# Inverses turned by VectorE, the mixer's output product on whole fp32 weights, and S5's input projections in pairs of row groups

## The chip, the cores and the metric

One NeuronCore of a Trainium2 chip runs the whole program as one launch. The metric is the time of an execution in device microseconds; lower is better. Before the change the median of three runs is 3645.67 us (3633.72 to 3649.02).

## What is computed

Two transformer blocks for 256 tokens of width 2048, all in fp32. The first is a hybrid mixer (sparse attention and a Mamba2 scan, both 1024 wide, whose results are joined and multiplied by `w_out`) and a product-key expert layer. The second has three branches of width 1024: a gated delta rule, RWKV-7 and a diagonal state-space model (S5). Cut to what the change touches:

```python
# first block: the mixer's output product, [256, 2048] @ [2048, 2048]
return jnp.concatenate([attn, ssm], axis=-1) @ w_out
# second block, S5: the input projections of every group of channels
bu_re = jnp.einsum('gpc,blgc->blgp', bb_re, ug)
bu_im = jnp.einsum('gpc,blgc->blgp', bb_im, ug)
# second block, delta rule: the inverse of a unit lower triangular matrix
t_mat = lax.linalg.triangular_solve(eye + lower, jnp.broadcast_to(eye, lower.shape),
                                    left_side=True, lower=True)
```

RWKV-7 is computed in chunks in the kernel, so it needs inverses of the same kind.

## The kernel before

**Weights in two parts.** A weight tile [128, 1024] is loaded by SyncE into a staging tile (`raw`, four of them, and two named `rawm` in the first block). ScalarE copies it, rounded, into `whi` (L280), VectorE subtracts that from the tile into `wlo` (L284), and TensorE forms three products of rounded operands (`mm3`, L291 to L293: high by high, high by low, low by high) or two where high and low of the activations lie side by side (`mm2`, L299 and L300). There are two pairs of `whi` and `wlo`, and a third while `self.third` names a pool. Such products (fp32r) are one record of TensorE; a product of fp32 operands is two records.

**Streams.** Weight products are generators in `self.queue`. `fill()` advances the first of them by one weight tile; the attention heads, the scans, S5 and the inverses call it between their own steps, so that products of weights stand between them on TensorE. `self.bg` is a second stream: the modulation weights (`ada`), 512 KB tiles that VectorE multiplies by the condition (L355) in the mixer's time. The framework then orders each engine's instructions itself; each engine runs them in that order.

**The mixer's output product** (`mixer`, `tm`). The attention's result is turned into `aT` (`chunk_T`, high part by ScalarE, low part by VectorE, L445) and multiplied by half of `w_out` in four groups of 512 columns, 4 weight tiles each, from 419 to 502 us beside the scan of the state-space half (`ssd`); that half's result is turned into `mT` and multiplied by the other half of the weights. The modulation stream runs beside both.

**S5** (`s5`). For each of 8 groups of 128 channels: the input matrices are turned (`pb`), and for each of four state tiles, which take 32 of those channels each, TensorE forms the real and the imaginary projection (L1729, L1730) in a bank of its own, VectorE rotates them (L1735, L1736), GpSimd joins them (L1737, L1738), VectorE scans (L1741), and `fill` puts two or three weight steps behind it. The pool `sm` has four banks.

**Inverses** (`inverse2`, called 16 times by `rwkv_pair` and 8 times by `gdn_pair`, two at a time through `both`). A call inverts two unit lower triangular matrices side by side, by doubling the block size from 1 to 64. In a step of block size b the off-diagonal blocks (`lb`, masked by GpSimd at L1790) are multiplied by the inverse so far, `Y` (L1805), `Y` is turned by TensorE (L1807), ScalarE copies both to SBUF (L1809), the two are multiplied (L1814), and VectorE subtracts the result from `Y` (L1815). Up to b = 32 `Y` consists of diagonal blocks no larger than 32 x 32 when it is turned. The start (L1798, L1800) turns the blocks of size 1 and subtracts them from the identity.

Of the kernel before, what the change touches and what calls it, by code (L numbers as in the profile page):

```python
# [7 lines left out]
F32 = mybir.dt.float32  # L8
F32R = mybir.dt.float32r
I32 = mybir.dt.int32  # L10
U32 = mybir.dt.uint32
AF = mybir.ActivationFunctionType
ALU = mybir.AluOpType
# [220 lines left out]
class K:  # L234
    def __init__(self, tc, A, at, dbg=None):
        self.tc, self.nc, self.A, self.at, self.dbg_ = tc, tc.nc, A, at, dbg
        self.n = 0
        self.pp, self.queue, self.done, self.bg = [], [], set(), []
        self.bgr, self.bgc = 1.0, 0.0
        self.side, self.later = [], [[] for _ in range(LAG)]  # L240
        self.third, self.ns = None, 0
        self.more, self.nr = None, 0

# [41 lines left out]

    def wt(self, src, n=1024, **kw):
        return self.split(self.raw(src, n), n, **kw)

    def mm3(self, out, shi, slo, mhi, mlo, start, stop):
        mm = self.nc.tensor.matmul  # L290
# [145 lines left out]
    def chunk_T(self, src, dg, hi, lo, scale, half=0):  # L436

        nc = self.nc
        if half == 0:
            self.ctb = self.bank()  # L440
        ps = self.ctb[:, half * S : half * S + S]
        for q in range(2):
            self.turn(ps[:, q * 128 : q * 128 + 128], src[q], dg and dg[q])
        nc.scalar.activation(hi, ps, AF.Copy, scale=scale)
        nc.vector.scalar_tensor_tensor(lo, ps, scale, hi.bitcast(F32), op0=ALU.mult, op1=ALU.subtract)  # L445

    def chunks_T(self, pool, x, cs, dg, hh, hl, scale, shift):

# [156 lines left out]
    def mixer(self, hp, mx, ax, hT, kvT, qT, xs, ev, scr):  # L605
# [31 lines left out]
        self.feed(*[self.cm(A["w1cm"], j, hT, lambda j, ps: ev((2 * NP + j + 8) % 12, ps), ("x", j)) for j in range(12 - 2 * NP)])  # L637
        self.feed(*[self.tm(A["w1z"], g, hT, self.gates(xs[2]), ("z", g)) for g in range(2)])
        atp = tc.alloc_tile_pool(name="atp", bufs=1, side="right")
        aT = [self.t(atp, [128, 8, S], F32R) for _ in range(2)]  # L640
        self.until("t320")
        gate = self.t(mx, [128, 2, 48])
        nc.scalar.activation(gate, vtm[:, :, 256:304], AF.Tanh, scale=0.5)
# [13 lines left out]
        nw = self.cp("attn_norm", "cp2")  # L657
        for c in range(8):
            a = [at[:, q, c * 128 : c * 128 + 128] for q in range(2)]
            self.chunk_T(a, None, aT[0][:, c], aT[1][:, c], nw[:, c : c + 1], c % 2)  # L660
        self.dbg("aTd", aT[0].bitcast(F32))
        ax.release()

        xp = tc.alloc_tile_pool(name="x1p", bufs=1)
# [20 lines left out]

        wo = lambda h: [A["wo1"][8 * g + 4 * h + i] for g in range(4) for i in range(4)]
        for g in range(4):
            self.feed(self.tm(wo(0), g, aT, ev_a, nk=8))
        assert not self.side
        self.until(*[("x", j) for j in range(12 - 2 * NP)])  # L690
        self.flush()
        turn, mT = self.ssd(mx, xs, hp)
        self.drain()
        for g in range(4):
            self.feed(self.tm(wo(1), g, mT, ev_m, nk=8))
        self.fill(3)
        for _ in turn:
            pass
        self.dbg("mTd", mT[0].bitcast(F32))
        self.drain()  # L700
        while self.bg:
            self.step_bg()
# [251 lines left out]
    def ssd(self, mx, xs, hp):  # L954

        nc = self.nc
        V, ACT, PL = nc.vector, nc.scalar, nc.gpsimd
        tri = self.cp("tri", "ca")
        xtm, bc, zs = xs
        dt, acs, acsT, ds = self.sd  # L960
        y = zs
        ss = self.t(mx, [128, 4])

        def scan(g, hg, cbT, py):
            h = g * 8 + hg
            pa = self.bank()
            nc.tensor.matmul(pa[:, 0:256], self.ident[:16, h : h + 1].to_broadcast([16, 128]), acsT, start=True, stop=True)
            seg = self.t(mx, [128, 384], tag="seg", bufs=2)
            ACT.activation(seg[:, 0:256], pa[:, 0:256], AF.Relu, scale=-1.0, bias=acs[:, 0, h : h + 1])
            ACT.activation(seg[:, 256:384], pa[:, 128:256], AF.Relu, scale=-1.0, bias=acs[:, 1, h : h + 1])  # L970
            ACT.activation(seg, seg, AF.Exp, scale=-1.0)
            V.scalar_tensor_tensor(seg[:, 0:256], seg[:, 0:256], dt[:, 0, h : h + 1], cbT[:, 0:256], op0=ALU.mult, op1=ALU.mult)
            V.scalar_tensor_tensor(seg[:, 256:384], seg[:, 256:384], dt[:, 1, h : h + 1], cbT[:, 256:384], op0=ALU.mult, op1=ALU.mult)
            yield
            o = slice(hg * 64, hg * 64 + 64)
            xc = slice(h * 64, h * 64 + 64)
            nc.tensor.matmul(py[0][:, o], seg[:, 0:128], xtm[:, 0, xc], start=True, stop=True)
            nc.tensor.matmul(py[1][:, o], seg[:, 128:256], xtm[:, 0, xc], start=True, stop=False)
            nc.tensor.matmul(py[1][:, o], seg[:, 256:384], xtm[:, 1, xc], start=False, stop=True)
            yield  # L980

        def turns(g, mT):
            nw = self.cp("ssm_norm", "cp2")
            for c in range(4 * g, 4 * g + 4):
                a = [y[:, q, c * 128 : c * 128 + 128] for q in range(2)]
                self.chunk_T(a, None, mT[0][:, c], mT[1][:, c], nw[:, c : c + 1], c % 2)
                if c % 2:
                    yield

        for g in range(2):  # L990
            ps = self.bank()
            Bt, Ct = bc[:, g], bc[:, 2 + g]
            nc.tensor.matmul(ps[:, 0:256], Bt[:, 0:128], Ct, start=True, stop=True)
            nc.tensor.matmul(ps[:, 256:384], Bt[:, 128:256], Ct[:, 128:256], start=True, stop=True)
            cbT = self.t(mx, [128, 384], tag="cbT", bufs=2)
            V.tensor_tensor(cbT[:, 0:256], ps[:, 0:256], tri, op=ALU.mult)
            V.tensor_tensor(cbT[:, 256:384], ps[:, 256:384], tri[:, :128], op=ALU.mult)
            py = [self.bank() for _ in range(2)]
            self.fill()
            gens = [scan(g, hg, cbT, py) for hg in range(8)]  # L1000
            if g:
                gens.insert(2, turn)
            self.weave(gens, 1, 0.17)
            self.until(("z", g))
            for q in range(2):
                c = slice(g * 512, g * 512 + 512)
                t1 = self.t(mx, [128, 512], tag="yd", bufs=2)
                PL.tensor_tensor(
                    t1.rearrange("p (h d) -> p h d", h=8), xtm[:, q, c].rearrange("p (h d) -> p h d", h=8),
                    ds[:, g * 8 : g * 8 + 8, None].to_broadcast([128, 8, 64]), op=ALU.mult,  # L1010
                )
                V.tensor_tensor(t1, py[q], t1, op=ALU.add)
                V.tensor_tensor(y[:, q, c], t1, zs[:, q, c], op=ALU.mult)
                ACT.activation(t1, y[:, q, c], AF.Square, accum_out=ss[:, 2 * q + g : 2 * q + g + 1])
            r = self.rstd(mx, ss[:, g::2], 2, 512.0, 4 * EPS)
            y0, y1 = (y[:, q, g * 512 : g * 512 + 512] for q in range(2))
            ACT.activation(y0, y0, AF.Copy, scale=r[:, 0:1])
            V.tensor_scalar(y1, y1, r[:, 1:2], None, op0=ALU.mult)
            if g == 0:
                self.until(("z", 1))  # L1020
                mT = self.pair(hp, 8, "hh")
            turn = turns(g, mT)
        return turn, mT

# [326 lines left out]
    def tm(self, wd, g, hT, evac, key=None, nk=NK):  # L1351

        hh, hl = hT[:2]
        ps = [self.t(self.acc, [128, 512], tag="acc") for _ in range(2)]
        for kp in range(nk // 2):
            hi, lo = self.wt(wd[g * (nk // 2) + kp])
            yield
            for k in range(2):
                kk = 2 * kp + k
                w = slice(k * 512, k * 512 + 512)  # L1360
                for q in range(2):
                    tk = slice(q * 128, q * 128 + 128)
                    self.mm3(ps[q], hh[:, kk, tk], hl[:, kk, tk], hi[:, w], lo[:, w], kk == 0, kk == nk - 1)
        for q in range(2):
            evac(g, q, ps[q])
        self.done.add(key)

    def step_bg(self):
        while self.bg:
# [320 lines left out]
    def s5(self, pl, u_, yT):  # L1690
# [19 lines left out]
        for j in range(8):  # L1710
# [11 lines left out]
            states = []  # L1722
            for i in range(4):
                sc = 4 * j + i
                P = slice(32 * i, 32 * i + 32)
                cs = self.r2()
                nc.sync.dma_start(cs, self.s5t[sc])
                pu = self.bank()
                nc.tensor.matmul(pu[:, 0:256], bT[P, 0:128], u[P], start=True, stop=True)  # L1729
                nc.tensor.matmul(pu[:, 256:512], bT[P, 128:256], u[P], start=True, stop=True)  # L1730

                w2 = lambda x: x.rearrange("p (w t) -> p w t", w=2)
                co, ns = (cs[:, None, o : o + 256].to_broadcast([128, 2, S]) for o in (0, 256))
# [44 lines left out]
    def inverse2(self, L, res):  # L1778
# [14 lines left out]

        lm, lb = masked(1), masked(2)
        yield
        ps = self.bank()
        for i in range(2):
            nc.tensor.transpose(ps[:, T[i]], lm[:, T[i]], self.ident)  # L1798
        Y = self.r1()
        V.tensor_tensor(v2(Y), id2, v2(ps[:, 0:256]), op=ALU.subtract)  # L1800
        yield
        for b in (2, 4, 8, 16, 32):
            ps = self.bank()
            for i in range(2):
                mm(ps[:, T[i]], lb[:, T[i]], Y[:, T[i]], start=True, stop=True)  # L1805
            for i in range(2):
                nc.tensor.transpose(ps[:, U[i]], Y[:, T[i]], self.ident)  # L1807
            zx = self.r2()
            nc.scalar.activation(zx, ps, AF.Copy)  # L1809
            if b < 32:  # L1810
                lb = masked(2 * b)
            yield
# [500 lines left out]
```

## Time and profile before

| | |
|---|---|
| median of 3 runs | 3645.67 us (3633.72 to 3649.02) |
| the profiled execution | 3638.32 us, span 3636.3 us |
| mean granted TensorE clock | 0.972 |
| TensorE matmul, weight load | 96%, 81% of the span |
| VectorE, ScalarE, GpSimd | 71%, 47%, 11% |
| read from HBM | 673.87 MB, 194 GB/s over the span |

The share of the matmul row holds each record's pipeline tail; how much a record takes from the next is read from the distance of their starts in the timeline. The stages that the change touches: the mixer's output product from about 402 to 565 us, S5 from 2217 to 2545, inverses of RWKV from 2596 to about 3110 and of the delta rule to about 3490.

### The profile page before, as it was taken

Reading aid. Unit: us, or ns where it says so; the run is one execution under the profiler, and the core shown is the slowest. Engines: PE = TensorE matmul, PEld = TensorE weight load, DVE = VectorE, ACT = ScalarE, POOL = GpSimd, SP = SyncE. Lnnn points to the kernel's source line nnn. Section 1 sums busy time; section 2 is a strip of 40 time slices with the busy share of each in tenths; the row PEclk is TensorE's granted clock in tenths of the full one; section 3 lists DMA queues with packets and bytes.
Section 4 is the critical chain, followed back from the end, with each engine's and each line's share of the span. In section 5 each row is a group of like instructions: output and inputs, shape, how many; then the busy total and the mean of one; then the engine's idle time right before and its main releaser. Section 6 shows DMA issues by size and latency. Waiting matters only on the chain. (4 is left out here: it accounts for less than half of the span.)

```text
span 3636.3 us, 53121 instructions
## 1 busy us (share of the span) xinstructions
PE 3473.7 (96%) x19334; PEld 2930.2 (81%) x19334; DVE 2570.2 (71%) x4552; ACT 1692.7 (47%) x2966; POOL 397.2 (11%) x487
## 2 busy tenths in 40 slices
PE   5899988999999999999999998999999999999998
PEld 4888767888998888778887877877888888778887
DVE  7777886798887755565577668989766666665665
ACT  2355544445554444445555554333544445444444
POOL 0000010000000000000000002333223222021310
PEclk7999988999999999999999998999999999999999
DMA  8965776666556865566788755645433433444455
GB/s 334 336 225 194 251 254 209 197 196 202 161 159 207 259 190 188 183 204 206 241 283 285 248 189 202 198 152 188 147 109 112 144 129 106 140 132 151 141 176 189
DMA packets 237298, 710.46 MB, mean 195 GB/s; under 512 B 34091, under 2 KB 61804, under 8 KB 235756
## 3 DMA queue, kind: packets, MB, share of 16 engines
q1 hardware_dynamic: 207564, 672.08, 56.7%
q10 hardware_dynamic: 29472, 34.98, 2.9%
q8 instruction: 152, 2.49, 0.3%
q14 instruction: 110, 0.90, 0.1%
HBM read 673.87 MB, written 32.55 MB: 194 GB/s over the span
## 5 line engine op out<-in xcount | busy, mean ns | idle before, releaser
L284 DVE TENSOR_TENSOR wlo<-raw,whi 128x1024 fp32r<-128x1024 f32 (+1 forms) x973 | 1216.8, 1251 | 595.2 <-ACT whi L280 591.1
L280 ACT ACTIVATE whi<-raw 128x1024 fp32r<-128x1024 f32 (+1 forms) x973 | 1017.7, 1047 | 1252.1 <-PE acc L293 577.2
L299 PE MATMUL acc<-hh,whi 128*128 128x512 f32 x3328 | 1195.2, 400 | 0.7 <-DVE cT L459 0.7
L300 PE MATMUL acc<-hh,wlo 128*128 128x256 f32 x3328 | 939.1, 282 | 7.0 <-DVE wlo L284 7.0
L299 PEld LDWEIGHTS acc<-hh,whi 128*128 128x128 f32 x3328 | 626.2, 188 | 143.3 <-issue 4.5
L300 PEld LDWEIGHTS acc<-hh,wlo 128*128 128x128 f32 x3328 | 629.2, 189 | 13.1 <-DVE wlo L284 11.7
L292 PE MATMUL acc<-wlo,wh 128*128 128x512 f32 x1024 | 402.8, 393 | 6.4 <-DVE wlo L284 5.5
L293 PE MATMUL acc<-whi,wl 128*128 128x512 f32 x1024 | 400.1, 391 | 0.0
L291 PE MATMUL acc<-whi,wh 128*128 128x512 f32 x1024 | 396.9, 391 | 3.3 <-DVE ge L1345 2.8
L291 PE MATMUL acc<-whi,hh 128*128 128x512 f32 (+1 forms) x672 | 273.7, 411 | 3.2 <-DVE r L1345 2.6
L292 PE MATMUL acc<-wlo,hh 128*128 128x512 f32 (+1 forms) x672 | 269.3, 401 | 7.3 <-DVE wlo L284 7.2
L293 PE MATMUL acc<-whi,hh 128*128 128x512 f32 (+1 forms) x672 | 267.0, 398 | 0.0
L292 PEld LDWEIGHTS acc<-wlo,wh 128*128 128x128 f32 x1024 | 192.9, 188 | 56.7 <-DVE wlo L284 16.5
L291 PEld LDWEIGHTS acc<-whi,wh 128*128 128x128 f32 x1024 | 192.7, 188 | 44.9 <-ACT wh L280 3.1
L293 PEld LDWEIGHTS acc<-whi,wl 128*128 128x128 f32 x1024 | 193.1, 189 | 39.5
L293 PE MATMUL acc<-hh,wlo 128*128 128x256 f32 x608 | 181.8, 299 | 13.6 <-DVE wlo L284 13.6
L291 PE MATMUL acc<-hh,whi 128*128 128x256 f32 x608 | 183.4, 302 | 5.2 <-ACT whi L280 3.3
L292 PE MATMUL acc<-hh,whi 128*128 128x256 f32 x608 | 179.0, 295 | 1.0 <-DVE hh L284 1.0
L291 PEld LDWEIGHTS acc<-whi,hh 128*128 128x128 f32 x672 | 129.7, 194 | 41.2 <-issue 11.8
L292 PEld LDWEIGHTS acc<-wlo,hh 128*128 128x128 f32 x672 | 130.8, 195 | 35.4 <-DVE wlo L284 10.9
L293 PEld LDWEIGHTS acc<-whi,hh 128*128 128x128 f32 x672 | 130.0, 194 | 27.4 <-issue 0.3
L1790 POOL TENSOR_TENSOR r<-r,cb 128x256 f32<-128x256 f32 x144 | 133.2, 945 | 162.6 <-DVE r L2123 37.5
(594 smaller groups left out, 5041.9 us busy)
## 6 DMA issues: line engine op xcount, KB each, us to landing
raw<-in_pu_dram SPq DMA_DIRECT2D x256, 512.0 KB, 3.9
raw<-in_pv_dram SPq DMA_DIRECT2D x252, 512.0 KB, 4.3
raw<-in_ada_dram SPq DMA_DIRECT2D x138, 512.0 KB, 5.1
raw<-in_w2gate_dram SPq DMA_DIRECT2D x96, 512.0 KB, 3.6
rawm<-in_ada_dram SPq DMA_DIRECT2D x54, 512.0 KB, 5.3
raw<-in_wo_dram SPq DMA_DIRECT2D x54, 512.0 KB, 4.3
raw<-in_w2br_dram SPq DMA_DIRECT2D x48, 512.0 KB, 3.5
raw<-in_w2g_dram SPq DMA_DIRECT2D x48, 512.0 KB, 3.5
```

The source lines that it names most:

```text
L280: nc.scalar.activation(hi, src, AF.Copy)
L284: self.lo = e.tensor_sub(lo, src, hi.bitcast(F32)).ins
L291: mm(out, shi, mhi, start=start, stop=False)
L292: mm(out, shi, mlo, start=False, stop=False)
L293: mm(out, slo, mhi, start=False, stop=stop)
L299: mm(out, hi, both, start=start, stop=False)
L300: mm(out[:, S:], lo, both[:, 0], start=False, stop=stop)
L1790: PL.tensor_tensor(v2(lb), v2(L), cb(f"M{b}"), op=ALU.mult)
```

## The change

1. `inverse2` turns `Y` (and the start's blocks) on VectorE, which transposes 32 x 32 blocks in place, into SBUF; TensorE's transposes go, and ScalarE copies 256 columns instead of 512.
2. `tm_whole` takes the place of `tm` for the mixer's output product: a weight tile is loaded (`whole`) straight into one of the tiles that the splits use and multiplied as fp32 by the turned activations, which are kept whole (`chunk_T` without a low part).
3. `s5` forms the projections of two state tiles together, their products in turn, in two banks.

```diff
+    def whole(self, src):
+
+        self.nw = (self.nw + 1) % (6 if self.third else 4)
+        p, n = (self.third, "3") if self.nw > 3 else (self.stg, "")
+        t = self.t(p, [128, 1024], F32R, tag=("whi", "wlo")[self.nw % 2] + n, bufs=1 if n else 2).bitcast(F32)
+        self.nc.sync.dma_start(t, src)
+        return t
...
-        nc.vector.scalar_tensor_tensor(lo, ps, scale, hi.bitcast(F32), op0=ALU.mult, op1=ALU.subtract)
+        if lo is not None:
+            nc.vector.scalar_tensor_tensor(lo, ps, scale, hi.bitcast(F32), op0=ALU.mult, op1=ALU.subtract)
...
-        aT = [self.t(atp, [128, 8, S], F32R) for _ in range(2)]
+        aT = self.t(atp, [128, 8, S])
...
-            self.feed(self.tm(wo(0), g, aT, ev_a, nk=8))
+            self.feed(self.tm_whole(wo(0), g, aT, ev_a, nk=8))
...
-            self.feed(self.tm(wo(1), g, mT, ev_m, nk=8))
+            self.feed(self.tm_whole(wo(1), g, mT, ev_m, nk=8))
...
+    def tm_whole(self, wd, g, hT, evac, nk):
+
+        ps = [self.t(self.acc, [128, 512], tag="acc") for _ in range(2)]
+        for kp in range(nk // 2):
+            w = self.whole(wd[g * (nk // 2) + kp])
+            yield
+            for k in range(2):
+                kk = 2 * kp + k
+                for q in range(2):
+                    self.nc.tensor.matmul(
+                        ps[q], hT[:, kk, q * 128 : q * 128 + 128], w[:, k * 512 : k * 512 + 512], start=kk == 0, stop=kk == nk - 1
+                    )
...
-                P = slice(32 * i, 32 * i + 32)
...
-                pu = self.bank()
-                nc.tensor.matmul(pu[:, 0:256], bT[P, 0:128], u[P], start=True, stop=True)
-                nc.tensor.matmul(pu[:, 256:512], bT[P, 128:256], u[P], start=True, stop=True)
+                if i % 2 == 0:
+
+                    pus = [self.bank() for _ in range(2)]
+                    for h in range(2):
+                        for k, pu in enumerate(pus):
+                            P = slice(32 * (i + k), 32 * (i + k) + 32)
+                            nc.tensor.matmul(pu[:, 256 * h : 256 * h + 256], bT[P, 128 * h : 128 * h + 128], u[P], start=True, stop=True)
+                pu = pus[i % 2]
...
-        ps = self.bank()
-        for i in range(2):
-            nc.tensor.transpose(ps[:, T[i]], lm[:, T[i]], self.ident)
+        V.tensor_tensor(v2(lm), id2, v2(lm), op=ALU.subtract)
         Y = self.r1()
-        V.tensor_tensor(v2(Y), id2, v2(ps[:, 0:256]), op=ALU.subtract)
+        V.transpose(Y, lm)
...
-            for i in range(2):
-                nc.tensor.transpose(ps[:, U[i]], Y[:, T[i]], self.ident)
             zx = self.r2()
-            nc.scalar.activation(zx, ps, AF.Copy)
+            nc.scalar.activation(zx[:, 0:256], ps[:, 0:256], AF.Copy)
+            V.transpose(zx[:, 256:512], Y)
```

**Where instructions move.** TensorE in a step of two joint inverses of RWKV, before (names: `sm` are the banks, `r` the inverses and their factors, `cs` the identity, `acc<-hh,whi` a weight product):

```order
L1805 MATMUL sm_23741<-r_4362_23558,r_4386_23671 128x128 x2
L1807 MATMUL sm_23741<-cs_63,r_4362_23558 128x128 x2
L1805 MATMUL sm_23750<-r_4364_23563,r_4389_23680 128x128 x2
L1807 MATMUL sm_23750<-cs_63,r_4364_23563 128x128 x2
L299 MATMUL acc_23706<-hh_19945,whi_23737 128x512
```

and the like place now:

```order
L1832 MATMUL sm_23405<-r_4296_23155,r_4335_23338 128x128 x2
L1832 MATMUL sm_23413<-r_4297_23158,r_4338_23346 128x128 x2
L1971 MATMUL sm_23421<-u_3617_19655,r_4355_23422 128x256
L1972 MATMUL sm_23421<-u_3617_19655,r_4355_23422 128x256
L308 MATMUL acc_23370<-hh_19544,whi_23401 128x512
```

The transposes (L1807) are gone; the second products of the step (L1814, now L1840) still follow after 16 rows of weight products. VectorE in the same step now (L1841 the subtractions, L1835 the transposes, L285 splits of weights):

```order
L1841 TENSOR_TENSOR r_4296_23155<-r_4296_23155,sm_23332 128x256
L1355 TENSOR_TENSOR r_4339_23364<-acc_23297,r_4339_23364 128x256
L1841 TENSOR_TENSOR r_4297_23158<-r_4297_23158,sm_23340 128x256
L1835 STREAM_TRANSPOSE r_4349_23408<-r_4296_23155 128x256
L1606 SCALAR_TENSOR_TENSOR r_4340_23367<-r_4340_23367,r_4339_23364 128x256
L285 TENSOR_TENSOR wlo_23475<-raw_23472,whi_23474 128x512
L1835 STREAM_TRANSPOSE r_4352_23416<-r_4297_23158 128x256
```

The second transpose stands behind the split of a half-sized weight tile. SyncE's queue where the mixer's output product begins, before:

```order
L266 DMA raw_3941<-in_ada_dram 128x1024
L266 DMA raw_3981<-in_wo_dram 128x1024
L266 DMA raw_4013<-in_wo_dram 128x1024
L266 DMA rawm_3987<-in_ada_dram 128x1024
L266 DMA raw_4019<-in_ada_dram 128x1024
```

and now:

```order
L267 DMA raw_3932<-in_ada_dram 128x1024
L267 DMA raw_3974<-in_ada_dram 128x1024
L267 DMA raw_3997<-in_ada_dram 128x1024
L295 DMA whi_3992<-in_wo_dram 128x1024
L295 DMA wlo_3972<-in_wo_dram 128x1024
L267 DMA rawm_3994<-in_ada_dram 128x1024
```

Two more loads of the modulation stream stand ahead of the product's first loads, which now wait for tiles named `whi` and `wlo`.

## Rows read from the trace of the kernel before

**Rows 1.** The page, busy time of each engine (us, share of the span, instructions)
```profile
PE 3473.7 (96%) x19334; PEld 2930.2 (81%) x19334; DVE 2570.2 (71%) x4552; ACT 1692.7 (47%) x2966; POOL 397.2 (11%) x487
```

**Rows 2.** The page, 40 slices: granted clock in tenths, transfer rate
```profile
PEclk7999988999999999999999998999999999999999
...
GB/s 334 336 225 194 251 254 209 197 196 202 161 159 207 259 190 188 183 204 206 241 283 285 248 189 202 198 152 188 147 109 112 144 129 106 140 132 151 141 176 189
```

**Rows 3.** Windows: stretch, length, busy per engine, granted clock, DMA share, GB/s
```profile
402.00:502.00 100.00, 96.36 (x437) 73.75 (x436) 83.18 (x113) 50.94 (x93) 15.18 (x12) 0.91 0.77 258
502.00:565.00 63.00, 51.86 (x191) 37.77 (x190) 52.56 (x55) 21.40 (x35) 4.36 (x4) 0.86 0.83 287
...
2217.00:2545.00 328.00, 308.93 (x1704) 246.59 (x1703) 288.34 (x377) 118.85 (x147) 117.94 (x104) 0.95 0.56 183
2545.00:3110.00 565.00, 546.38 (x3515) 465.13 (x3515) 360.27 (x660) 262.49 (x557) 149.42 (x208) 0.99 0.38 122
3110.00:3500.00 390.00, 382.11 (x2161) 318.51 (x2160) 241.79 (x402) 182.65 (x347) 79.01 (x99) 0.99 0.44 143
```

**Rows 4.** Waits, 402 to 592 us and, SyncE's queue, 402 to 565
```profile
ACT whi L280 <- DMA raw<-in_wo_dram: 22.7, 9, 5.1
...
SPq L266 <- DVE wlo L284: 60.1, 32, 5.0
```

**Rows 5.** Groups by line and form, TensorE: busy, mean ns, idle before
```profile
L1807 PE MATMUL sm<-cs,r 128*128 128x128 f32 x240 | 46.3, 275 | 0.0
L291 PE MATMUL acc<-whi,u 128*128 128x512 f32 x64 | 27.0, 437 | 0.0
```

**Rows 6.** Timeline of TensorE, one joint step of RWKV: start us, us
```profile
3025.89 0.71 PE L1805 MATMUL sm<-r,r 128*128 128x128 f32 x4
3026.44 0.38 PE L1807 MATMUL sm<-cs,r 128*128 128x128 f32 x2
3026.66 0.61 PE L1805 MATMUL sm<-r,r 128*128 128x128 f32 x4
3027.10 0.38 PE L1807 MATMUL sm<-cs,r 128*128 128x128 f32 x2
3027.24 0.48 PE L299 MATMUL acc<-hh,whi 128*128 128x512 f32 x1
...
3030.11 1.05 PE L1814 MATMUL sm<-r 128*128 128x128 f32 x8
```

**Rows 7.** Groups by line and form, VectorE's transposes
```profile
L396 DVE STREAM_TRANSPOSE adr<-adt 128x1024 f32<-128x1024 f32 x2 | 2.5, 1239 | 0.0
...
L410 DVE STREAM_TRANSPOSE u<-u 32x64 f32<-32x64 f32 x1 | 0.2, 226 | 0.0
```

**Rows 8.** Groups by line and form, VectorE's splits
```profile
L284 DVE TENSOR_TENSOR wlo<-raw,whi 128x1024 fp32r<-128x1024 f32 x945 | 1191.5, 1261 | 581.1 <-ACT whi L280 577.0 <-PE sm L1798 3.5
```

**Rows 9.** Timeline of TensorE, the projections of one state tile in S5
```profile
2461.17 0.69 PE L1729 MATMUL sm<-mA,r 32*128 32x256 f32 x2
2461.71 0.59 PE L1730 MATMUL sm<-mA,r 32*128 32x256 f32 x2
2462.23 0.50 PE L291 MATMUL acc<-whi,hh 128*128 128x512 f32 x1
```

**Rows 10.** Timeline of TensorE, RWKV: products in turn on two row groups
```profile
2587.40 1.16 PE L2008 MATMUL sm<-r,r 64*128 64x128 f32 x16
2588.49 0.39 PE L300 MATMUL acc<-hh,wlo 128*128 128x256 f32 x1
```

**Rows 11.** Timeline, the mixer's output product: two records, three between them
```profile
480.15 0.40 PE L291 MATMUL acc<-whi,u 128*128 128x512 f32 x1
...
481.30 0.40 PE L293 MATMUL acc<-whi,u 128*128 128x512 f32 x1
```

**Rows 12.** Timeline and source line: fp32 products of 512 columns
```profile
266.68 1.88 PE L745 MATMUL sm<-raw,ca 128*128 128x512 f32 x4
...
L745 PE MATMUL sm<-raw,ca x16: 590/592/1219, 163.6 to 318.6; 128*128 128x512 f32 x16
```

More of the change, by code (lines that the diff above doesn't have):

```diff
@@ L240, in __init__ @@
         self.side, self.later = [], [[] for _ in range(LAG)]
+        self.nw = 0
         self.third, self.ns = None, 0
@@ L659, in mixer @@
             a = [at[:, q, c * 128 : c * 128 + 128] for q in range(2)]
-            self.chunk_T(a, None, aT[0][:, c], aT[1][:, c], nw[:, c : c + 1], c % 2)
-        self.dbg("aTd", aT[0].bitcast(F32))
+            self.chunk_T(a, None, aT[:, c], None, nw[:, c : c + 1], c % 2)
+        self.dbg("aTd", aT)
         ax.release()
@@ L698, in mixer @@
             pass
-        self.dbg("mTd", mT[0].bitcast(F32))
+        self.dbg("mTd", mT)
         self.drain()
@@ L985, in turns @@
                 a = [y[:, q, c * 128 : c * 128 + 128] for q in range(2)]
-                self.chunk_T(a, None, mT[0][:, c], mT[1][:, c], nw[:, c : c + 1], c % 2)
+                self.chunk_T(a, None, mT[:, c], None, nw[:, c : c + 1], c % 2)
                 if c % 2:
@@ L1020, in ssd @@
                 self.until(("z", 1))
-                mT = self.pair(hp, 8, "hh")
+                mT = self.t(hp, [128, 8, S], tag="hh")
             turn = turns(g, mT)
@@ L1366, in tm @@
         self.done.add(key)
+    def tm_whole(self, wd, g, hT, evac, nk):
[9 more added lines that the diff above has]
+                    )
+        for q in range(2):
+            evac(g, q, ps[q])
     def step_bg(self):
```

## The prediction

> **What bounds the kernel now.** I read the shares of the page first. TensorE's matmul row is busy for 3473.7 of 3636.3 us, VectorE for 2570.2, ScalarE for 1692.7 [rows 1] and its clock is granted in full in most slices [rows 2]. A busy matmul row holds pipeline tails, so the second look is at the stretches in which the change lies [rows 3]. From 402 to 502 us, the first half of the mixer's output product, TensorE is busy for 96.4 of 100 us at a mean granted clock of 0.91; from 502 to 565, the second half, for 51.9 of 63 at 0.86; in S5 (2217 to 2545) for 308.9 of 328 at 0.95, with VectorE at 288.3 beside it; in the RWKV stretch (2545 to 3110) for 546.4 of 565 at 0.99 with VectorE at 360.3; in the delta-rule stretch (3110 to 3500) for 382.1 of 390 at 0.99 with VectorE at 241.8. So in the last two TensorE is the bound and VectorE has about a third of its time free; in S5 both are near their limit; in the mixer neither is full, and the third look, at the waits, says what stops it: ScalarE waited 22.7 us for weight tiles of this product to land, and the load queue held its next load back for 60.1 us until VectorE had finished a split and freed the staging tile [rows 4]. A mean clock of 0.91 between two levels, 1.2 and 2.4 GHz, means that 18% of that stretch ran at the lower one.
>
> **Turned inverses.** `inverse2` runs 24 times, 16 in RWKV and 8 in the delta rule. Each loses 10 TensorE transposes in its five steps (L1807, 240 in all [rows 5]) and 2 at its start (L1798, 48). Their mean of 275 ns is mostly tail; what one takes from the next is the distance of starts: of the four in one step two hold TensorE from 3026.44 to 3026.66 and two from 3027.10 to 3027.24 [rows 6], 0.36 us in all, 0.09 each. 288 x 0.09 = 26 us, by the slower pair alone 32; I take 28. In their place VectorE gets 144 transposes of 128x256. The trace has a VectorE transpose of 1024 columns, 1.239 us, and one of 64, 0.226 us [rows 7]; on a line between them 256 columns cost an estimated 0.43 us, in all 62 us. VectorE's 602 us in the two stretches become 664 of 955, 70%: it stays behind TensorE. The Trainium skill has a price of its own, in "VectorE: DVE Perf Modes", section "The three transpose paths": 311 ns for a 128x128 block on VectorE, 390 ns on TensorE, for bf16. By it the 144 (two blocks each) would be an estimated 90 us, VectorE would stand at 72%, and TensorE's share and the sum would be the same; the fp32 rows of this trace decide.
>
> On the path of a step lie the product of L1805, the copy to SBUF, the product of L1814 and the subtraction; the copy now takes half the columns, and the transpose runs beside the first product and the copy. In the step shown, the first products start at 3025.89 and the second at 3030.11, 4.2 us later, with one weight tile's products between them [rows 6]; that work is the cover of a transpose of 0.43 us. What is exposed is the order on VectorE: of the 120 transposes of the steps, 58 stand behind at least one weight split (1.26 us, [rows 8]) after the subtraction that makes their input. I take 25 us of the 28 as gain, 17 of them in RWKV. Ends: 32, all of it and somewhat shorter waits, and 7, if every second of the 60 joint steps loses 0.7 us, about half a split, to a late transpose (28 - 30 x 0.7). The 24 subtractions at the start read SBUF in place of PSUM, in the same size, and I cost that at nothing; they come ahead of a transpose where they came behind one, and the weight products that fill the step cover them either way.
>
> **S5's projections.** A state tile's four records (two products, two records each) hold TensorE from 2461.17 to 2462.23, 1.06 us [rows 9]; 32 tiles, 34 us. The change lets the products of two tiles alternate between two groups of 32 rows. The nearest row for that is L2008, which alternates two groups of 64 rows: 16 records of 128 columns in 1.09 us [rows 10], 0.068 each, where records of that size that follow on all 128 rows need 0.14 at L1805 (four from 3025.89 to 3026.44 [rows 6]): the pairs run at the same time but for a head at each entry. So two tiles should need about 1.06 us instead of 2.12, and 16 x 1.06 = 17 us are saved. But VectorE is busy for 88% of this stretch [rows 3] and a tile's chain runs through it, so I count 10. Ends: 18 (TensorE alone decides, and less is lost to the low clock) and 0 (VectorE decides). The second bank is taken earlier by one tile; the pool has four, and each is emptied by VectorE before its turn comes again, so I cost that at nothing.
>
> **The mixer's product.** Removed: 384 records at 0.23 us (from 480.15 to 481.30 there are five, 1.15 us [rows 11]), 64 per line for the first half [rows 5], the same for the second: 88 us. Added: 128 fp32 products, which are two records each: the four records of two such products at L745 last 1.88 us in all, and one 0.59, so (1.88 - 0.59)/3 = 0.43 us from start to start [rows 12]. 256 x 0.43 = 110 us. TensorE gets 22 us more. VectorE loses 32 splits of 1.26 us, 40 us, and 16 low halves of turned chunks; ScalarE loses the 32 high halves. Each load now goes straight into one of six tiles that the splits used, and the staging tiles are left to the other stream (the modulation weights). On the load queue the first direct load stands behind two more loads of the other stream and waits until a product of the gate's last weights has released its tile; every later one waits for the products of the tile six before it, and the modulation loads queue behind it. Between that release and its own use lie the products of five tiles, 5 x 8 x 0.43 = 17 us; ScalarE's longest wait for a landing in that row was 5.1 us [rows 4], so the queue should stay ahead.
>
> In the 163 us TensorE is idle for 15, and the clock costs half of some 18 + 17.6 us at the lower level [rows 3]: about 32 us are there to take up 22. The load waits lose their cause (a split), and VectorE falls from 135.7 busy to some 93. I forecast 4 us less. Ends: 14 less (all idle time and half of the clock's loss go), and 18 more (the idle time stays and the 22 come on top).
>
> **Sum.** Against the profiled execution, 3638.3 us with a span of 3636.3: -25 - 10 - 4 = -39, 3599. The median of the runs before is 3645.7, 7 above that execution; so 3606 as a median.
>
> **Rivals.** (a) The mixer keeps its idle time and pays the 22 us: 3645.7 - 25 - 10 + 18 = 3629. For it: modulation loads of equal size compete for the transfers (258 and 287 GB/s in these stretches, 334 and 336 in the kernel's first slices [rows 2, 3]), which a faster TensorE can't hurry. Against: the cause of its waits is VectorE's splits [rows 4]. (b) S5 is held by VectorE: 3645.7 - 25 - 4 = 3617. For it 288 of 328 busy; against, TensorE's 309. (c) **Slower**: late transposes. If VectorE's order puts a split ahead of a transpose and TensorE stands in front of L1840 until it comes, a joint step loses up to 1.26 us; 60 of them lose 76 us, and 3606 becomes 3682. It decides from (39 + 18)/60 = 0.95 us a step on. Against it stand the 4.2 us between the two products of a step [rows 6], three times a split. (d) The row groups don't run at the same time, since 32-row records of 256 columns are not 64-row ones of 128: S5 then changes by nothing, which is the time of (b).
>
> **Chances.** Forecast 0.62, (a) 0.15, (b) with (d) 0.16, (c) 0.06, and 0.01 for anything else. The bounds together reach from 3645.7 - 32 - 18 - 14 = 3582 to 3645.7 - 7 - 0 + 18 = 3657; that all terms fall at one end is unlikely, so the range is 3580 to 3634, which holds the forecast, (b) and most of (a). About 0.5% (18 us) is what a measurement of this kernel can tell from no change. Faster by over that (below 3627): the forecast, (b) and a small part of (a), 0.78. Within it: most of (a) and of the forecast's bad end, 0.16. Slower: (c), 0.06.
>
> **What would show it.** Right: no L1807 or L1798, 144 transposes of some 0.43 us on VectorE, the RWKV stretch from its first to its last inverse about 17 us shorter and the delta rule's about 8; starts of S5's records in pairs a few ns apart and the stretch to 2545 some 10 us shorter beyond what the mixer shifts it; 256 records of 0.43 us in the mixer, with a granted clock above 0.91 and hardly a wait for `wo` to land. Wrong: TensorE waiting for VectorE's transposes (rival c), S5's length unchanged with VectorE above 90% (b), or the mixer's stretch longer than 163 us (a).

## The result, and the profile after

The changed kernel takes 3597.9 us (median of four runs, 3586.7 to 3605.4) where the kernel before, run beside it, takes 3642.2: a ratio of 0.9882, 95% interval 0.9854 to 0.9910, or 44 us less (33 to 53). A second set of runs gave 3596.5 us and 0.9886 (0.9864 to 0.9909). The profiled execution took 3600.3 us, with a span of 3598.2.

The first lines of the page after, which answer to [rows 1, 2]:

```profile
PE 3427.4 (95%) x18918; PEld 2852.2 (79%) x18918; DVE 2565.5 (71%) x4648; ACT 1632.8 (45%) x2934; POOL 390.3 (11%) x487
...
PEclk7999999999999999999999999999999999999999
```

TensorE lost 46 us of busy time and ScalarE 60; VectorE stands where it stood, though it lost 32 splits and got 144 transposes. The lower clock that two slices of the mixer showed is gone.

Where the time went is read by stage, not from the shares. The four stages that the change touches, from the same matmul to the same matmul in both traces: the mixer's output product up to the first query projection; S5; RWKV up to its last matmul; the delta rule up to the first chunk turned behind it. The columns are those of the first line; the number in brackets counts instructions. First the kernel before:

```profile
core 0: us, PE busy (x) PEld busy (x) DVE busy (x) ACT busy (x) POOL busy (x), PEclk, DMA share, GB/s
419.20:592.40 173.20, 150.55 (x643) 115.11 (x642) 138.48 (x174) 73.14 (x130) 19.00 (x17) 0.87 0.75 256
...
2217.40:2554.60 337.20, 317.15 (x1747) 252.28 (x1746) 296.87 (x386) 121.64 (x150) 122.16 (x110) 0.95 0.56 183
...
2554.60:3115.50 560.90, 542.23 (x3495) 462.83 (x3494) 354.07 (x656) 263.19 (x567) 146.78 (x208) 0.99 0.38 121
3115.50:3502.20 386.70, 379.83 (x2146) 316.55 (x2145) 241.25 (x400) 179.82 (x332) 77.42 (x93) 0.99 0.45 144
```

and the same four after:

```profile
419.60:578.10 158.50, 151.69 (x515) 80.35 (x513) 98.48 (x133) 42.56 (x98) 22.31 (x17) 0.98 0.77 276
...
2205.80:2540.80 335.00, 296.39 (x1748) 239.84 (x1747) 283.37 (x386) 121.17 (x150) 119.78 (x110) 0.97 0.56 184
...
2540.80:3080.40 539.60, 523.21 (x3328) 444.04 (x3325) 386.11 (x752) 246.32 (x568) 141.89 (x208) 1.00 0.39 127
3080.40:3465.80 385.40, 372.09 (x2036) 308.52 (x2034) 260.74 (x447) 169.52 (x333) 76.02 (x93) 0.97 0.44 144
```

The mixer gave 14.7 us, S5 2.2, RWKV 21.3, the delta rule 1.3. The stretch between the mixer and S5, which the change does not touch, went from 1625.0 to 1627.7, and the last one is 1.8 us shorter. So the total came out as forecast (39 us on the profiled executions, 38 found), and its parts did not: the mixer gave almost 4 times its term, S5 hardly anything.

These views say how. The inverses' transposes, with the time of one and who waited for them (view of their line in the change):

```profile
L1835 DVE STREAM_TRANSPOSE r<-r x120: 395/435/446, 2587.5 to 3442.9; 128x256 f32<-128x256 f32 x120
...
who waited for it (us, times):
  PE sm L1840: 1.3, 2
```

One takes 0.435 us, the estimate was 0.43, and TensorE waited for two of the 120.

S5's pairs, TensorE's timeline of one:

```profile
2205.83 1.13 PE L1758 MATMUL sm<-mA,r 32*128 32x256 f32 x8
2206.89 0.39 PE L300 MATMUL acc<-hh,whi 128*128 128x256 f32 x1
```

Eight records hold TensorE for 1.06 us from their first start to the next matmul's, which four did before [rows 9]; their starts come in twos 7 ns apart. The two groups of rows do run at the same time, and TensorE's busy time in S5 fell by 21 us. But its waits for splits in that stage, before:

```profile
PE acc L293 <- DVE wlo L284: 1.9, 4, 0.6
...
PE acc L292 <- DVE wlo L284: 0.5, 2, 0.3
```

and after:

```profile
PE acc L301 <- DVE wlo L285: 14.7, 12, 2.4
PE acc L302 <- DVE wlo L285: 13.6, 10, 2.3
```

grew from 2.4 us to 28.3, while its other waits fell: by the windows it is idle for 38.6 us of the stage instead of 20.1. It now stands still for VectorE's splits instead. The mixer's new products, by their line:

```profile
L1387 PE MATMUL acc<-wlo,u x64: 590/592/697, 419.6 to 497.4; 128*128 128x512 f32 x64
```

start 429 ns after one another in the median (256 of them, 114 us with their few longer steps).

### The profile page after: what moved, and what is told of

Read it like the earlier page. It is cut to its first block, busy times and chain, and to the rows that moved or that the text cites. A ratio compares the mean times of both kernels' runs of the same rounds, so it can differ in the third digit from the quotient of the medians.

```text
span 3598.2 us, 52389 instructions
## 1 busy us (share of the span) xinstructions
PE 3427.4 (95%) x18918; PEld 2852.2 (79%) x18918; DVE 2565.5 (71%) x4648; ACT 1632.8 (45%) x2934; POOL 390.3 (11%) x487
## 5 line engine op out<-in xcount | busy, mean ns | idle before, releaser
L285 DVE TENSOR_TENSOR wlo<-raw,whi 128x1024 fp32r<-128x1024 f32 (+1 forms) x951 | 1167.8, 1229 | 567.1 <-ACT whi L281 562.8
L281 ACT ACTIVATE whi<-raw 128x1024 fp32r<-128x1024 f32 (+1 forms) x951 | 994.0, 1046 | 1224.8 <-PE acc L302 577.3
L309 PEld LDWEIGHTS acc<-hh,wlo 128*128 128x128 f32 x3328 | 629.6, 189 | 13.5 <-DVE wlo L285 12.0
L301 PE MATMUL acc<-wlo,hh 128*128 128x512 f32 (+1 forms) x608 | 243.7, 401 | 14.9 <-DVE wlo L285 14.7
L300 PE MATMUL acc<-whi,hh 128*128 128x512 f32 (+1 forms) x608 | 248.1, 409 | 5.3 <-DVE r L1355 5.3
L302 PE MATMUL acc<-whi,hh 128*128 128x512 f32 (+1 forms) x608 | 242.1, 398 | 0.0
L301 PEld LDWEIGHTS acc<-wlo,hh 128*128 128x128 f32 x608 | 118.3, 195 | 43.1 <-DVE wlo L285 21.1
L302 PEld LDWEIGHTS acc<-hh,wlo 128*128 128x128 f32 x608 | 122.0, 201 | 34.0 <-DVE wlo L285 31.9
L364 DVE SCALAR_TENSOR_TENSOR ada<-raw,u,ada 128x1024 f32<-128x1024 f32 x101 | 131.7, 1304 | 21.6 <-DMA raw<-in_ada_dram 20.7
```

Of the source, the lines that this page charges most:

```text
L281: nc.scalar.activation(hi, src, AF.Copy)
L285: self.lo = e.tensor_sub(lo, src, hi.bitcast(F32)).ins
L300: mm(out, shi, mhi, start=start, stop=False)
L301: mm(out, shi, mlo, start=False, stop=False)
L302: mm(out, slo, mhi, start=False, stop=stop)
L309: mm(out[:, S:], lo, both[:, 0], start=False, stop=stop)
```

## The experiments

**The three edits alone.** Each is one part of the change on the kernel before; the lines that mark it:

```diff
@@ e_inv: inverse2 @@
-                nc.tensor.transpose(ps[:, U[i]], Y[:, T[i]], self.ident)
...
+            V.transpose(zx[:, 256:512], Y)
@@ e_s5: s5 @@
-                nc.tensor.matmul(pu[:, 0:256], bT[P, 0:128], u[P], start=True, stop=True)
...
+                        for k, pu in enumerate(pus):
@@ e_mix: the mixer @@
-            self.feed(self.tm(wo(0), g, aT, ev_a, nk=8))
+            self.feed(self.tm_whole(wo(0), g, aT, ev_a, nk=8))
```

> The kernel before with the turned inverses alone. Reading of the two traces (A): the RWKV stretch went from 551.9 to 530.6 us and the delta rule's from 395.7 to 394.4, so the inverses alone should give about -22 us (ratio 0.994), nearly all of it in RWKV, and the delta rule's stretch should stay within 3 us of before. The prediction's split (B): -17 in RWKV and -8 in the delta rule. Told apart by the two stretches, not by the sum. Should (A) hold, the place of the loss is the step from RWKV to the delta rule: there 14 rows of projection matmuls stand between the last sum of squares and the first product with the roots where 40 stood before, so TensorE should wait 4 to 5 us for the root's last VectorE step, and run at half its clock for some 10 us behind it.

> The kernel before with S5's pairs alone. Reading of the traces (A): VectorE holds this stage, so the 17 us that leave TensorE turn into waits for VectorE's splits, and the stage shortens by about 2 us: ratio 0.9995, stage 335 us against 337. The prediction's sum (B): -10 us, ratio 0.997, stage 327. Under A the waits of the projections on wlo in this stage grow from 2.4 us to about 28.

> The kernel before with the mixer's whole weights alone. Reading of the traces (A): -14 us, ratio 0.996; the stretch from 402 us to the first query projection shortens from 190 to 176. The prediction's sum (B): -4 us, ratio 0.999. Rival (C): part of the 14 us comes from the other two edits, by an order of instructions that changes with them; then this kernel gains less than 10.

Measured: e_inv 0.995 (0.9933 to 0.9968), 18 us less; e_s5 1.000 (0.9988 to 1.0012); e_mix 0.9959 (0.9943 to 0.9975), 15 us less. The stages in us, from their traces:

| stage | before | e_inv | e_s5 | e_mix | the change | the change again |
|---|---|---|---|---|---|---|
| mixer's product to query | 173.2 | 169.5 | 165.8 | 157.6 | 158.5 | 159.5 |
| S5 | 337.2 | 336.9 | 336.4 | 337.8 | 335.0 | 336.1 |
| RWKV | 560.9 | 538.6 | 559.6 | 558.1 | 539.6 | 538.6 |
| delta rule | 386.7 | 383.1 | 389.8 | 383.5 | 385.4 | 381.3 |

Each stage moves with its own edit; that the mixer's gain came from the other two edits, the rival (C) of e_mix, is not borne out, as e_mix alone has all of it. The mixer without its edit lies at 166 to 173, with it at 158 to 160, so the profile of before was at the long end and the edit is worth 6 to 16 us there. The delta rule without turned inverses is 384 to 390, with them 381 to 385: some 4 us. TensorE's busy time did fall there as it should, from 379.8 to 370.6 us in e_inv, but its idle time rose from 6.9 to 12.6. S5's pairs give nothing that can be measured; reading A stands as far as TensorE goes, with 28.1 us of TensorE's waits on splits in e_s5 (12 + 10 waits). That VectorE holds the stage is read from such waits; no run takes work from VectorE there. The sum of the three, 33 us, lies at the end of the whole's interval; that the edits help one another is not shown.

**What made the mixer faster: the long fp32 records or the missing splits?** One kernel leaves out the low parts of weights and activations, and with them VectorE's splits, and puts the old records back; the other keeps the new records and the splits:

```diff
@@ e_hi3: tm_whole @@
-            w = self.whole(wd[g * (nk // 2) + kp])
+            src = self.raw(wd[g * (nk // 2) + kp])
...
+            self.nc.scalar.activation(w, src, AF.Copy)
...
+                    self.mm3(ps[q], x, x, v, v, kk == 0, kk == nk - 1)
@@ c_keep: tm_whole @@
-            w = self.whole(wd[g * (nk // 2) + kp])
+            w = self.raw(wd[g * (nk // 2) + kp])
+            self.split(w)
```

> The change with the mixer's product taken as three fp32r matmuls of the rounded weights (made by ScalarE alone) instead of one in fp32; the low part of weights and activations is left out and the high product stands three times, so that TensorE has the same records as in the kernel before, and VectorE no split. Theory A, the long fp32 records keep TensorE at work and its clock up: without them the clock falls again, the stretch from 402 us to the first query projection stays within 6 us of the kernel before's 190 and the granted clock is near 0.88. Theory B, the splits on VectorE and the waits behind them were the cost: then TensorE's 22 us less of records show in the end time, the stretch is some 155 us and the kernel 20 us faster than the change, ratio 0.982 to 0.984. Between them: both matter, stretch about 170.

> The change with the mixer's 32 weight tiles still loaded as raw tiles and still split by ScalarE and VectorE, though only the whole tile is multiplied, in fp32 as in the change. Theory A: what the whole weights took away is VectorE's and ScalarE's splits with the waits behind them (from the first output product to the first query projection the kernel before took 166 to 173 us, the change 158, and the three fp32r matmuls without VectorE's split 158 too); then this one goes back to 166 to 173 us and the kernel is 8 to 15 us slower than the change, ratio 0.990 to 0.992. Theory B: TensorE's long fp32 records keep the clock up, whatever the other engines do: then the stretch stays within 3 us of 158 and the ratio at 0.988.

Measured: e_hi3 0.9912 (0.9891 to 0.9934), c_keep 0.9952 (0.9936 to 0.9968). The stretch in e_hi3:

```profile
423.60:581.60 158.00, 140.30 (x643) 110.37 (x641) 98.34 (x133) 72.79 (x130) 22.58 (x17) 0.91 0.77 278
```

and in c_keep, with waits of ScalarE and of the load queue:

```profile
419.00:595.50 176.50, 159.14 (x516) 84.57 (x514) 132.71 (x163) 72.80 (x131) 20.61 (x17) 0.93 0.73 250
...
ACT whi L281 <- DMA raw<-in_wo_dram: 29.5, 11, 5.5
...
SPq L267 <- PE acc L1388: 74.3, 23, 12.1
```

With the old records and no split on VectorE the stretch is 158.0 us, as in the change; with the new records and the splits it is 176.5, more than the 166 to 173 of the old product. So the gain comes from VectorE's split and the staging tile that waits for it, and not from the long fp32 records: e_hi3 has a clock of 0.91 and 18 us of idle TensorE, the change a clock of 0.98 and 7 us idle, and both need the same time for the stretch. The change's 22 us of extra records fit into idle time and low clock. Neither experiment met its figures. For e_hi3 theory B asked for 20 us less than the change; by the ratios the kernel is some 10 us slower (the intervals overlap), and in the profiled executions that difference lies outside the stretch. For c_keep theory A asked for 8 to 15 us more than the change, and the kernel takes some 24 more. Two things stay joined: c_keep holds each staging tile until the products are through (the load queue waited for them 74.3 us, once 12.1; in the change its loads waited 70.1 us for products, at most 5.3 at once), so it does not tell the split's work from the tile's holding. Nor is it shown what keeps e_hi3 from ending earlier; 19.4 us of its ScalarE's waits are for weights to land, and from 415 to 560 us transfers run at 302 to 307 GB/s in it and at 324 and 284 in the change, not far from the 345 of the fastest slice of the page after. Whether transfers now hold both is not tested.

**How much cover the transposes have.**

```diff
             V.transpose(zx[:, 256:512], Y)
+            V.transpose(zx[:, 256:512], Y)
```

(and the same for the 24 at the start.)

> The change with each of VectorE's 144 transposes of the inverses made twice, 62 us more on VectorE (41 of it in RWKV, 21 in the delta rule), each second one right behind the first. Theory A (the transposes are hidden beside the matmuls of the same step): under 6 us in all, ratio 0.988 to 0.990. Rival C of the prediction (the transpose lies on the path of every step): 0.43 us for each of the 60 joint steps is 26 us, ratio 0.995, and TensorE waits for the transposes' lines.

Measured: 0.9901 (0.9885 to 0.9918), against 0.9882 and 0.9886 for the change in its two sets. Its windows of RWKV and the delta rule, and TensorE's wait at the second product of a step:

```profile
2543.50:3085.20 541.70, 525.19 (x3337) 444.32 (x3334) 415.40 (x849) 248.20 (x570) 140.11 (x208) 1.00 0.40 127
3085.20:3466.50 381.30, 368.14 (x2024) 304.98 (x2022) 273.43 (x494) 169.80 (x331) 76.14 (x93) 0.97 0.45 144
...
PE sm L1842 <- DVE r L1837: 2.3, 4, 0.9
```

RWKV grew by 2 to 3 us, the delta rule by nothing, and TensorE waited for four transposes. By the ratios the whole is 5 to 7 us, which is within the intervals. Theory A holds: the 26 us of the other are not there.

**The hand-over to the delta rule.** In the change TensorE waits there once for long and runs at half its clock from 3141 us on for 17 of the next 27 us; its wait, from the view of waits:

```profile
PE sm L2201 <- DVE rsy L2184: 4.8, 1, 4.8
```

With the turned inverses the order of work has 14 rows of projections there instead of 40. The experiment asks for more:

```diff
         gd["rs"] = rs
+        self.fill(4)
```

> The change with four steps of projection work asked for at the hand-over from RWKV to the delta rule, so that 34 rows of projection matmuls instead of 14 stand between the last sum of squares and the first product with the roots (40 in the kernel before). Theory A: the wait of 4.8 us and the 17 us at half clock behind it are what kept the delta rule from gaining what its transposes cost; the stage shortens by 5 to 9 us, ratio 0.9855 to 0.987. Theory B: the matmuls are only moved, and are missing later in the stage: no difference, ratio 0.988.

Measured: 0.9895 (0.9878 to 0.9912). That wait is gone and the stage is 380.4 us long, against 381.3 to 385.4; the time shows no difference. The half clock did not go with the wait: from 3143 us on it stands for 14 of the next 27 us, whose mean is 0.75 (0.69 in the change). Theory B: the matmuls are moved, and another wait, of 3.1 us for a transpose at an inverse's start, stands 20 us later in the stage. That the hand-over is what kept the delta rule from its forecast gain is not shown.

**What holds S5.** VectorE is busy for 283 of 335 us and waits for GpSimd in three rows of its waits in the change:

```profile
DVE r L1770 <- POOL r L1766: 17.8, 27, 0.9
DVE r L1773 <- POOL r L1771: 12.6, 11, 1.2
...
DVE r L1773 <- POOL r L1893: 4.3, 4, 1.2
```

Three versions try to fill these 35 us with other work: the two tiles' steps interleaved, the splits asked for between the steps of a tile, and the latter with VectorE's order fixed.

```diff
@@ s5_interleaved: s5 @@
+                for k in range(2):
...
+                    V.tensor_tensor(w2(a), w2(pus[k]), co, op=ALU.mult)
...
+                for k, (a, b, co, ns) in enumerate(ab):
...
+                        V.tensor_tensor_scan(w[:, h], mg, a[:, h], 0.0, op0=ALU.mult, op1=ALU.add)
@@ s5_spread: s5 @@
+                self.fill()
                 mg = self.mag[:, sc : sc + 1].to_broadcast([128, S])
...
                 V.tensor_tensor(w2(a), w2(w), co, op=ALU.mult)
+                self.fill()
...
-                self.fill(3 if sc % 4 else 2)
+                if sc % 4:
+                    self.fill()
@@ s5_forced: s5_spread, and the same behind the second product @@
+                pm_ = V.tensor_tensor(w2(a), w2(w), co, op=ALU.mult)
+                with self.tc.issue_after(pm_.ins):
+                    self.fill()
+                with self.tc.issue_after(self.lo):
+                    V.tensor_tensor(a[:, 0:256], a[:, 0:256], b[:, 256:512], op=ALU.add)
```

> The change with the elementwise work of S5's two state tiles interleaved: both tiles' four products first, then both tiles' scans, then the last sums, so that VectorE has the other tile's work while GpSimd finishes one. Theory A: VectorE is S5's limit, 283 us busy of 335 and 35 us of it waiting for GpSimd; with that wait gone the stage shortens by 15 to 30 us, the kernel is near 3575, ratio 0.980 to 0.984, and VectorE's busy share of the stage rises above 88%. Theory B: the stage is held by the splits' order or by the twelve wide buffers, which are all in use at a group's first pair: then the waits for GpSimd turn into waits for buffers or table loads, and the stage stays within 5 us of 335 (ratio 0.988), or gets longer.

Measured: 0.9996 (0.9982 to 1.0009), some 40 us slower than the change. VectorE's waits show GpSimd nowhere in the stage, and this stands in its place (waits of VectorE and TensorE, and the stage's window):

```profile
DVE wlo L285 <- ACT whi L281: 61.4, 36, 3.6
...
PE acc L301 <- DVE wlo L285: 38.4, 10, 4.4
...
2205.00:2578.30 373.30, 314.34 (x1747) 257.24 (x1746) 300.34 (x386) 119.82 (x150) 107.28 (x110) 0.90 0.50 166
```

Theory B in its "longer" form: TensorE stands still up to 4.4 us for splits, the clock falls to 0.90, and VectorE waits 61.4 us for ScalarE's halves, against 7.2 in the change. That the blocks for two tiles make the splits bunch is a reading of these waits; no run tests it apart. Nor did the time with GpSimd all go. The products behind the scans, first in the change and then here, show where most of it went:

```profile
L1772 DVE TENSOR_TENSOR r<-r,r 128x512 f32<-128x512 f32 x32 | 29.5, 922 | 0.8
...
L1776 DVE TENSOR_TENSOR r<-r,r 128x512 f32<-128x512 f32 x32 | 55.5, 1734 | 0.0
```

Here all 32 start while GpSimd multiplies and take 1.73 us each; in the change 7 do, and the other 25 take 0.69. So 26 of the 35 us of waits came back as longer products.

> The change with S5's projection steps asked for between the steps of a state tile (one after the products that GpSimd joins, one after the scans, one at the end) instead of three at the end, so that a split of weights stands on VectorE where it waits for GpSimd. Theory A: VectorE's order is S5's limit: it waits 35 us for GpSimd in the stage, of which about two thirds (20 us) find a split in their place; the stage shortens by 10 to 20 us, ratio 0.983 to 0.985. Interleaving the tiles took the same wait away and gathered VectorE's own work in long blocks, so that the splits came in bunches and the stage grew by 39 us; here no block grows. Theory B: the projections' buffers hold the stage, whatever VectorE's order; then within 4 us of the change.

> The version with the spread steps and the four steps of projection work at the hand-over to the delta rule together. If the hand-over is worth the 3 to 5 us that its stage showed (380 us against 381 to 385), this is 2 to 5 us below the spread version; if that was within the spread of runs, no difference.

> The change itself once more, to stand beside the versions below on the same chip: ratio 0.988, about 3598 us. Were the parts measured alone (0.995, 1.000, 0.9959) simply to add, it would be 0.991.

Measured: s5_spread 0.9892 (0.9873 to 0.9912), with the hand-over 0.9896 (0.9877 to 0.9914), the change beside them 0.9886 (0.9864 to 0.9909): no difference between the three. s5_spread did not do what it was made for. The scheduler put scans straight behind the products for more tiles than before and VectorE's waits for GpSimd stayed at 35 us, so it tells nothing on theory A. The next one fixes the order.

> The spread version with VectorE's order fixed: in S5 a split of weights is put behind the second product of every state tile and one behind its last scan's product, so that in all 32 tiles neither scans nor sums stand right behind what GpSimd has to work on. In the change 8 scans and 17 sums of the 32 stood so, in the spread version 14 and 19, and there the waits for GpSimd stayed at 35 us against 34, which is why its time says nothing about them. Theory A: with the waits for GpSimd down from 34 us to under 12 the stage shortens by 10 to 20 us, ratio 0.983 to 0.986. Theory B: the waits fall, and their time comes back as waits for splits and their slots (as when the tiles were interleaved): stage within 4 us of 336, or longer.

Measured: 0.9962 (0.9950 to 0.9974), some 28 us slower than the change; the stage takes 359.2 us. The waits for GpSimd did fall, to 13.8 us and not under 12, and others came (VectorE's waits, its group of splits, and the stage's window):

```profile
DVE r L1764 <- PE sm L1758: 23.6, 14, 3.7
DVE r L1773 <- POOL r L1766: 13.8, 22, 0.6
DVE r L1744 <- PE sm L1742: 10.5, 6, 4.0
...
L285 DVE TENSOR_TENSOR wlo<-raw,whi 128x1024 fp32r<-128x1024 f32 x89 | 140.3, 1578 | 2.9 <-ACT whi L281 2.9
...
2209.20:2568.40 359.20, 311.71 (x1747) 247.59 (x1746) 301.14 (x386) 121.15 (x150) 130.92 (x110) 0.95 0.52 172
```

The splits' mean rose from 1.29 to 1.58 us. The timelines of VectorE and GpSimd at one of them say why:

```profile
2224.24 2.31 DVE L285 TENSOR_TENSOR wlo<-raw,whi 128x1024 fp32r<-128x1024 f32 x1
...
2223.68 1.79 POOL L1774 TENSOR_TENSOR r<-r,r 128x512 f32<-128x512 f32 x1 [1.21 <-DVE r L1773]
```

The split takes 2.31 us and ends 1.08 us after GpSimd, which is done at 2225.47. In this stage 33 of 89 splits last over 1.5 us, with a median of 2.30. Each of them starts inside an instruction of GpSimd and ends 1.08 to 1.09 us behind it, whether that one lasts 0.7 or 1.8 us, so the split gets going when GpSimd is done. The others have a median of 1.21. In the change 7 of 88 are so long, in the kernel before 25 of 88. So GpSimd's time can't be covered with splits: a wait for GpSimd is exchanged for a split that waits inside. The Trainium skill has the rule, in "SBUF — State Buffer", section "Who interferes with whom": an instruction of VectorE with two inputs in SBUF contends with one of GpSimd that reads SBUF, for ports that are held under an exclusive lock. The trace agrees, at 1.1 us for each split.

That is why nothing was won; the stage's growth lies elsewhere. VectorE's busy time rose by 18 us and its waits for GpSimd fell by 21, but its waits for TensorE rose from 8 us to 34 in the view of waits. Why these rose is not shown.

Added up, the waits for GpSimd and what splits and products lose inside its instructions (their time over 1.21 and 0.69 us) are 47 us of S5 in the kernel before, 49 in the change and 48 in s5_forced, and the rest of VectorE's busy time is 267 to 269 us in all three. The pairs and the fixed order only changed whether this time shows as waits or as long instructions. None of the versions beats the change.

## Why the prediction was right, and where it was not

The forecast (3606 us, range 3580 to 3634, faster by over 0.5%) held; the median came out 8 us below it. Taken by its own steps:

- **Turned inverses, -25** ("17 of them in RWKV"): 18 us (12 to 24) alone. The number of transposes, their price on VectorE (0.43 forecast, 0.435 found) and the cover of 4.2 us were right. The split between the stages was not: 18 to 22 us in RWKV against 17, about 4 in the delta rule against 8. What the text did not count is that the order of work is made anew: the delta rule's matmuls lost 9 us of TensorE's time as they should, and 6 us of it came back as idle time, with a wait of 4.8 us at the hand-over among it. As filling that wait gave nothing in the time, the cause of the missing 4 us stays open.
- **S5's projections, -10**: nothing (interval -4 to +4). The step "two tiles should need about 1.06 us instead of 2.12" was right to the hundredth. The step that failed is "I count 10": with VectorE busy for 88% the text took a middle between its ends, and the stage kept to the end of rival (b), in which VectorE decides. What the text lacked is the chain: in the change 283 us of VectorE's work, 35 of waiting for GpSimd and 7 for ScalarE make 325 of 335. The sign that it gave for (b), VectorE above 90%, did not come (85%): waiting for GpSimd is no busy time.
- **The mixer's product, -4**: 15 us less (9 to 21), the good end of its range. The 429 ns per record (0.43 forecast) were right. The step that failed is "about 32 us are there to take up 22": it took what is lost to idle time and clock from 163 us, up to 565. The stretch that counts runs to the first query projection: 173 us with 22.7 idle, at a mean clock of 0.87, which is some 44 us at the lower level and so another 22 lost. About 45 us were there, not 32. The idle time fell by 15.8 us. The busy time rose by 1.1 only: the 22 us more of records stand against some 19 us less lost at a clock of 0.98 (7 us at the lower level). The mechanism, "the load waits lose their cause (a split)", is what e_hi3 and c_keep showed. Rival (a) is out: it held that a faster TensorE can't hurry the transfers, and they went faster (276 against 256 GB/s).
- **The sum**: that the total fits is in part luck. Taken alone, the inverses gave 7 us less than their term, S5 10 less and the mixer 11 more, 33 us in all; the whole gave 42 to 44, and where the rest comes from is not shown. A total that fits was no proof of its terms; only the stages and the edits taken one by one show that.
- **Rivals (c) and (d)** are out: the first by doubled transposes that cost RWKV 2 to 3 us and the whole 5 to 7, where (c) needs 0.95 us in each of 60 steps, the second by starts 7 ns apart and eight records in the time of four.

## What to carry to other kernels

Look for the engine on which a stage's chain lies, its waits for its partners and its instructions of unusual length included, before work is taken from another: 21 us left TensorE in S5 and came back as waits, while 40 us off VectorE in the mixer paid for 22 us more on TensorE and 15 besides. Work moved to an engine with a third of its time free was nearly free here, where something else lies beside each step, and doubling it was the quick way to know. And when an order of work is made anew by a scheduler, compare stage by stage: the sum hides both misses and gifts.

## What the runs showed that was not expected

- A VectorE split, which has two SBUF inputs, takes 2.30 us instead of 1.21 when it starts inside a GpSimd product of 128x512. The kernel before lost 26 us of VectorE's time to that in S5, the change 7; the pairs alone moved the splits, and the stage did not get shorter for it.
- Interleaving removed every wait of S5's VectorE for GpSimd from the view of waits and made the stage 38 us longer; 26 us of the waits came back inside VectorE's products.
- The last stretch, from the first chunk turned to the start of the last matmul, is 120.3 to 120.6 us in every version with turned inverses and 122.1 in the others, though it has no inverse in it. That was not followed up.
